# The second half of an input on ScalarE's DMA queue, and neighbouring channel blocks in one PSUM bank

## The chip, the core and the metric

The kernel runs on one core of a Trainium2 chip. The metric is the time of one execution on the device, in microseconds (us); the median of three runs of the kernel before is 260.43 us, with 260.27 and 260.7 us as the lowest and the highest. The engines are called PE (TensorE, matrix products), ACT (ScalarE), DVE (VectorE), POOL (GpSimd) and SP (SyncE, which issues transfers here). PE writes its results to PSUM, which ACT and DVE read; a bank of PSUM holds 512 fp32 values for each of 128 partitions.

## What is computed

The reference is one layer of an encoder block on an input `x` of 256 tokens by 1024 channels, in fp32. Cut to what matters:

```python
h = _rmsnorm(x, norm_gain)                 # x * rsqrt(mean(x*x) + eps) * gain
z = h @ w_in                               # 1024 x 8192, one combined projection
a_in, a_gate, q, k, v, b_gp, g_logits = jnp.split(z, splits, axis=-1)
y_a = (_multiscale_pool(a_in, w_pool, pool_scale) * silu(a_gate)) @ w_proj_a
y_b = (_dilated_attention(q, k, v, rel_bias) * silu(b_gp)) @ w_proj_b
merged = sigmoid(g[0]) * y_a + sigmoid(g[1]) * y_b
y = _rmsnorm(x + merged @ w_out, final_gain)
```

The change lies in what leads up to the first product `h @ w_in`: the load of `x`, its norm, and its transposition to channels by tokens.

## The kernel before, in words

Every fp32 product is made as three products of parts: a matrix is cut into a rounded high part and the rest (`hh` and `hl` for the activations, `whi` and `wlo` for weights), and `hh*whi`, `hl*whi` and `hh*wlo` are accumulated in PSUM. The weights come in 1 MB blocks `wraw` (256 output columns by 8 blocks of 128 input channels), four of them in flight, all issued by SP. ACT makes `whi` by a copy (L128), DVE makes `wlo` by a subtraction (L133).

The head of the program, the part that the change touches, runs before any of the projections and goes like this.

1. SP issues the two halves of `X` (128 tokens by 1024 channels each, L70), then weight block 0 in two halves (L110), weight block 1, the table `oh` and weight block 2 (L112, L147). ACT's queue carries one small transfer, `prm` (L78), with the norm's gains among others.
2. PE runs matmuls on zeros (L179) meanwhile. For each half b of the tokens ACT and DVE square and sum half of the channels each (L185, L187), DVE adds the two sums (L190), and POOL raises the result to -0.5 (L191). Then DVE and ACT scale half of the channels each: XN, channels 0 to 511 by DVE (L194), 512 to 1023 by ACT (L195).
3. DVE makes `whi` of weight block 0 in two copies (L197), each when its half has landed, and POOL makes its `wlo` in two pieces (L163).
4. PE turns XN in 16 pieces of 128 by 128 (`turn`, L204): block `kc` of the channels, half `b` of the tokens. The results go to four tiles `tps`, each one PSUM bank with room for two blocks of channels by 256 tokens.
5. For each block `kc` from 0 to 7 ACT reads the turned block from PSUM, times the gain, and writes `hh[kc]` (L223); then DVE reads the same block and writes `hl[kc] = block * gain - hh[kc]` (L224). PE multiplies as these come (`part0`, L213): pass A is `hh[kc]*whi`, two matmuls for each block, pass B is `hl*whi`, two blocks behind, and pass C is `hh*wlo`, which comes when A and B are through. In the midst of C stand six small matmuls on `oh` (L237).

The part from 2 to 5 stands in a hand-written order: ACT, DVE, PE and POOL carry out their instructions in the order of the code. What a semaphore must be waited for is worked out by the framework from the tiles that instructions touch; for PSUM it orders two engines that touch the same tile, two readers as well.

After the head PE goes through the projections, three matmuls for each block and output (L247, L248, L249), from line 247 on without a break; the pieces of attention are mixed in between.

Of the kernel before, what the change touches and what calls it, by code (L numbers as in the profile page):

```python
# [17 lines left out]
P = 128  # L18
# [24 lines left out]
def encoder_block(ctx: ExitStack, tc: tile.TileContext, x, w_in, lines, w_pool, w_proj_a, w_proj_b,  # L43
                  w_out, final_gain, params, out):
    nc = tc.nc
    x2 = x[0]
# [6 lines left out]
    def slot(shape, dt, tag, name, bufs=1):  # L53
        return sb.tile(shape, dt, tag=tag, name=name, bufs=bufs)
# [6 lines left out]
    def bank(shape, tag, name, bufs):  # L61
        return ps.tile(shape, F32, tag=tag, name=name, bufs=bufs)
# [4 lines left out]

    X = slot([P, 2, D], F32, "v", "X", 2)
    for b in range(2):
        nc.sync.dma_start(X[:, b, :], x2[b * P:(b + 1) * P, :])  # L70
    ident = sb.tile([P, P], F32, name="ident")
    make_identity(nc, ident)
    mhalf = sb.tile([P, 1], F32, name="mhalf")
# [62 lines left out]
    def cut_next():  # L136
        cut_half()
        cut_half()
# [16 lines left out]
    XN = slot([P, 2, D], F32, "v", "XN", 2)  # L155
# [5 lines left out]
    def cut_lo(n, k0, k1, eng):  # L161
        t, (hi, lo) = raws[n][0], parts[n]
        return eng.tensor_tensor(lo[:, k0:k1, :], t[:, k0:k1, :], hi[:, k0:k1, :].bitcast(F32), op=ALU.subtract)  # L163

    def open_parts(n):
        shp = raws[n][1]
        parts[n] = (slot([P] + shp, F32R, "whi", f"whi{n}", 3), slot([P] + shp, F32R, "wlo", f"wlo{n}", 3))
        state["cut"] = 2 * n + 2

    with tc.manual_schedule(engines={mybir.EngineType.Activation, mybir.EngineType.DVE, mybir.EngineType.PE,  # L170
                                    mybir.EngineType.Pool}):
        tiny = sb.tile([P, 1], F32, name="tiny")
        warm = sb.tile([P, P], F32, name="warm")
        nc.vector.memset(warm, 0.0)
        nc.scalar.activation(tiny, warm[:, 0:1], AF.Square)

        def keep_warm(times):
            for _ in range(times):
                nc.tensor.matmul(misc[:, P:2 * P], warm, warm, start=True, stop=True)  # L179

        keep_warm(WARM)
        halves = [slice(h * 512, (h + 1) * 512) for h in range(2)]
        for b in range(2):
            sq = [slot([P, 512], F32, "st", f"sq{b}{h}", 3) for h in range(2)]
            nc.scalar.activation(sq[0], X[:, b, halves[0]], AF.Square, scale=1.0 / 32.0, accum_out=ss[:, b, 0:1])  # L185
            xb = X[:, b, halves[1]]
            nc.vector.tensor_tensor_reduce(sq[1], xb, xb, scale=1.0 / D, scalar=EPS, op0=ALU.mult, op1=ALU.add,  # L187
                                           accum_out=ss[:, b, 1:2])
            t = slot([P, 1], F32, "rt", f"rt{b}", 2)
            nc.vector.tensor_tensor(t, ss[:, b, 0:1], ss[:, b, 1:2], op=ALU.add)  # L190
            nc.gpsimd.tensor_tensor(rs[:, b:b + 1], t, mhalf, op=ALU.pow)  # L191
        open_parts(0)
        for b in range(2):
            nc.vector.tensor_scalar(XN[:, b, halves[0]], X[:, b, halves[0]], rs[:, b:b + 1], None, op0=ALU.mult)  # L194
            nc.scalar.activation(XN[:, b, halves[1]], X[:, b, halves[1]], AF.Copy, scale=rs[:, b:b + 1])  # L195
        for k in (0, 4):
            nc.vector.tensor_copy(parts[0][0][:, k:k + 4, :], raws[0][0][:, k:k + 4, :])  # L197

        cut_lo(0, 0, 5, nc.gpsimd)
        first_lo = cut_lo(0, 5, 8, nc.gpsimd)  # L200
        tps = [bank([P, 2, S], "mm" if i < 3 else "T", f"tp{i}", 3 if i < 3 else 2) for i in range(4)]

        def turn(kc, b):
            nc.tensor.transpose(tps[kc % 4][:, kc // 4, b * P:(b + 1) * P], XN[:, b, kc * P:(kc + 1) * P], ident)  # L204

        acc = bank([P, 2, 512], "S", "k00", 1)
        acc0 = [acc[:, u, 0:S] for u in range(2)]

        def part0(kc, x):
            hi_, lo_ = parts[0]  # L210
            for u in range(2):
                c = slice(u * P, (u + 1) * P)
                nc.tensor.matmul(acc0[u], (lo_ if x == 2 else hi_)[:, kc, c], (hl if x == 1 else hh)[:, kc, :],  # L213
                                 start=x == 0 and kc == 0, stop=x == 2 and kc == KC - 1)

        for kc in range(KC):
            turn(kc, 0)
        for kc in range(KC):
            turn(kc // 2 + kc % 2 * 4, 1)
        for kc in range(KC):  # L220
            v = tps[kc % 4][:, kc // 4]
            gcol = prm[:, kc:kc + 1]
            nc.scalar.activation(hh[:, kc, :], v, AF.Copy, scale=gcol)  # L223
            nc.vector.scalar_tensor_tensor(hl[:, kc, :], v, gcol, hh[:, kc, :].bitcast(F32), op0=ALU.mult,  # L224
                                           op1=ALU.subtract)
            part0(kc, 0)
            if kc >= 2:
                part0(kc - 2, 1)
        for kc in (6, 7):
            part0(kc, 1)  # L230
        for kc in range(KC):
            if kc == 5:

                for t in range(3):
                    w = 3 * NH
                    o = 3 * P + t // 2 * w
                    nc.tensor.matmul(misc[:, t * w:(t + 1) * w], oh[:, t * P:(t + 1) * P], oh[:, o:o + w],  # L237
                                     start=True, stop=True)
            part0(kc, 2)
        cut_next()  # L240
        nc.vector.tensor_copy(line.rearrange("p i r h -> p r i h"),
                              misc[:, 0:LROW * NH].rearrange("p (r i h) -> p r i h", i=2, h=4))
        cut_next()
# [579 lines left out]
```

## Time and profile before

| | |
|---|---|
| median of 3 runs | 260.43 us (260.27 to 260.7) |
| the profiled execution's own time | 260.82 us |
| span of its profile | 259.0 us |
| PE busy | 250.4 us, 97% of the span |
| DVE busy | 210.2 us, 81% |
| ACT busy | 164.4 us, 63% |
| POOL busy | 74.5 us, 29% |
| first matmul of the projections (L247) | at 15.83 us |

The span runs from the first to the last instruction of the program; 1.8 us of the execution's own time lie around it. A row of the timeline has the start in us, the duration in us, the engine, the line, the operation, the tiles written and read, the shapes and a count; what stands in brackets at its end is the idle time of the engine just before, with what ended it. Rows of one kind that follow each other on an engine are merged into one row with their count. Buffers' numbers are left out in the profile: all four `tps` tiles are called `tp`.

### The profile page before, as it was taken

Reading aid. Unit: us, or ns where it says so; the run is one execution under the profiler, and the core shown is the slowest. Engines: PE = TensorE matmul, PEld = TensorE weight load, DVE = VectorE, ACT = ScalarE, POOL = GpSimd, SP = SyncE. Lnnn points to the kernel's source line nnn. Section 1 sums busy time; section 2 is a strip of 40 time slices with the busy share of each in tenths; the row PEclk is TensorE's granted clock in tenths of the full one; section 3 lists DMA queues with packets and bytes.
Section 4 is the critical chain, followed back from the end, with each engine's and each line's share of the span. In section 5 each row is a group of like instructions: output and inputs, shape, how many; then the busy total and the mean of one; then the engine's idle time right before and its main releaser. Section 6 shows DMA issues by size and latency. Waiting matters only on the chain.

```text
span 259.0 us, 5482 instructions
## 1 busy us (share of the span) xinstructions
PE 250.4 (97%) x2160; PEld 248.8 (96%) x2160; DVE 210.2 (81%) x412; ACT 164.4 (63%) x285; POOL 74.5 (29%) x101
## 2 busy tenths in 40 slices
PE   7899999999999999999999999999999999999990
PEld 7899999999999999999999999999999999999990
DVE  2899988778888787889697997967859988899383
ACT  4878577565666565658967777765457797446141
POOL 1563386002798000010763910000010020442011
PEclk9999999999999999999999999999999999999998
DMA  6999999984445553444989867144440696300022
GB/s 231 393 412 363 239 323 329 313 306 162 166 162 172 235 172 156 162 164 162 284 254 257 278 216 273 47 164 162 164 162 6 209 383 233 148 4 0 0 84 81
DMA packets 9992, 52.01 MB, mean 201 GB/s; under 512 B 1147, under 2 KB 2142, under 8 KB 4718
## 3 DMA queue, kind: packets, MB, share of 16 engines
q1 hardware_dynamic: 7022, 44.08, 48.4%
q0 software_dynamic: 2512, 7.12, 11.1%
q10 hardware_dynamic: 432, 0.46, 0.5%
q8 instruction: 17, 0.28, 0.4%
q14 instruction: 9, 0.07, 0.1%
HBM read 47.42 MB, written 1.09 MB: 187 GB/s over the span
## 4 chain that ended last, share of the span: by engine, by line
PE 84%; DVE 6%; issue 3%; ACT 2%; DMA 2%; POOLq 0%; POOL 0%; SPq 0%; DVEq 0%; ACTq 0%
PE v L249 4%; PE v L248 4%; PE q L249 4%; PE q L248 4%; PE v L247 4%; PE q L247 4%; PE g L247 4%; PE g L248 4%; PE g L249 4%; PE k L247 4%; PE k L249 4%; PE k L248 4%; PE y L247 2%; PE y L248 2%; PE y L249 2%
## 5 line engine op out<-in xcount | busy, mean ns | idle before, releaser
L133 DVE TENSOR_TENSOR wlo<-wraw,whi 128x512 fp32r<-128x512 f32 (+2 forms) x134 | 108.5, 849 | 8.3 <-ACT whi L128 7.3
L128 ACT ACTIVATE whi<-wraw 128x1024 fp32r<-128x1024 f32 (+1 forms) x80 | 81.0, 1038 | 23.2 <-PE q L248 10.1
L247 PE MATMUL g<-hh,whi 128*128 128x256 f32 x128 | 35.8, 280 | 0.0
L249 PE MATMUL g<-hh,wlo 128*128 128x256 f32 x128 | 35.4, 277 | 0.0
L248 PE MATMUL g<-hl,whi 128*128 128x256 f32 x128 | 35.4, 276 | 0.0
L304 ACT ACTIVATE st<-st,nm 128x512 f32<-128x512 f32 x16 | 11.6, 722 | 29.6 <-DVE nm L301 29.6
L247 PE MATMUL v<-whi,hh 128*128 128x256 f32 x96 | 26.6, 277 | 0.0
L249 PE MATMUL v<-whi,hl 128*128 128x256 f32 x96 | 26.5, 276 | 0.0
L248 PE MATMUL v<-wlo,hh 128*128 128x256 f32 x96 | 26.5, 276 | 0.0
L249 PE MATMUL q<-hh,wlo 128*128 128x256 f32 x96 | 26.5, 276 | 0.0
L247 PE MATMUL q<-hh,whi 128*128 128x256 f32 x96 | 26.5, 276 | 0.0
L248 PE MATMUL q<-hl,whi 128*128 128x256 f32 x96 | 26.5, 276 | 0.0
L247 PEld LDWEIGHTS g<-hh,whi 128*128 128x128 f32 x128 | 24.0, 188 | 0.1
L248 PEld LDWEIGHTS g<-hl,whi 128*128 128x128 f32 x128 | 24.1, 188 | 0.0
L249 PEld LDWEIGHTS g<-hh,wlo 128*128 128x128 f32 x128 | 24.0, 188 | 0.0
L247 PE MATMUL k<-hh,whi 128*128 128x256 f32 x80 | 22.2, 277 | 0.0
L249 PE MATMUL k<-hh,wlo 128*128 128x256 f32 x80 | 22.1, 277 | 0.0
L248 PE MATMUL k<-hl,whi 128*128 128x256 f32 x80 | 22.1, 277 | 0.0
L248 PEld LDWEIGHTS v<-wlo,hh 128*128 128x128 f32 x96 | 18.0, 188 | 0.0
L249 PEld LDWEIGHTS q<-hh,wlo 128*128 128x128 f32 x96 | 18.0, 188 | 0.0
L248 PEld LDWEIGHTS q<-hl,whi 128*128 128x128 f32 x96 | 18.0, 188 | 0.0
L247 PEld LDWEIGHTS q<-hh,whi 128*128 128x128 f32 x96 | 18.0, 188 | 0.0
(177 smaller groups left out, 760.2 us busy)
## 6 DMA issues: line engine op xcount, KB each, us to landing
wraw<-in_w_in_dram SPq DMA_DIRECT2D x31, 1024.0 KB, 6.4
wraw<-in_w_out_dram SPq DMA_DIRECT2D x4, 1024.0 KB, 4.9
T<-line_d POOLq DMA_DIRECT2D x4, 576.0 KB, 6.8
KX<-KX POOLq DMA_DIRECT2D x8, 256.0 KB, 14.5
wraw<-in_w_proj_a_dram SPq DMA_DIRECT2D x2, 1024.0 KB, 4.7
wraw<-in_w_proj_b_dram SPq DMA_DIRECT2D x2, 1024.0 KB, 4.9
X<-in_x_dram SPq DMA_DIRECT2D x2, 512.0 KB, 4.2
wraw<-in_w_in_dram SPq DMA_DIRECT2D x2, 512.0 KB, 6.6
```

Source lines behind the costliest of these rows:

```text
L128: nc.scalar.activation(hi[:, s, :], t[:, s, :], AF.Copy)
L133: nc.vector.tensor_tensor(lo[:, s, :], t[:, s, :], hi[:, s, :].bitcast(F32), op=ALU.subtract)
L247: nc.tensor.matmul(acc, ah, bh, start=first, stop=False)
L248: nc.tensor.matmul(acc, ah, bl, start=False, stop=False)
L249: nc.tensor.matmul(acc, al, bh, start=False, stop=last)
L304: e = nc.scalar.activation(st, st, AF.Exp, bias=nm, scale=-1.0, accum_out=l)
```

## The change

Three lines. The load of the second half of `X` is issued by ACT's queue, ahead of `prm`, where it was issued by SP. And the turned blocks are laid out otherwise in the four banks: before, block `kc` shared its bank with block `kc + 4` (`tps[kc % 4]`), now blocks 0 and 1 share the first bank, 2 and 3 the second, and so on (`tps[kc // 2]`). The pieces of the second half of the tokens are turned in the order 0, 1, 2, ... 7, where the order was 0, 4, 1, 5, 2, 6, 3, 7. The order in which ACT and DVE read the blocks is 0 to 7 in both.

```diff
     for b in range(2):
-        nc.sync.dma_start(X[:, b, :], x2[b * P:(b + 1) * P, :])
+        (nc.sync, nc.scalar)[b].dma_start(X[:, b, :], x2[b * P:(b + 1) * P, :])
...
         def turn(kc, b):
-            nc.tensor.transpose(tps[kc % 4][:, kc // 4, b * P:(b + 1) * P], XN[:, b, kc * P:(kc + 1) * P], ident)
+            nc.tensor.transpose(tps[kc // 2][:, kc % 2, b * P:(b + 1) * P], XN[:, b, kc * P:(kc + 1) * P], ident)
...
         for kc in range(KC):
             turn(kc, 0)
         for kc in range(KC):
-            turn(kc // 2 + kc % 2 * 4, 1)
+            turn(kc, 1)
         for kc in range(KC):
-            v = tps[kc % 4][:, kc // 4]
+            v = tps[kc // 2][:, kc % 2]
             gcol = prm[:, kc:kc + 1]
             nc.scalar.activation(hh[:, kc, :], v, AF.Copy, scale=gcol)
             nc.vector.scalar_tensor_tensor(hl[:, kc, :], v, gcol, hh[:, kc, :].bitcast(F32), op0=ALU.mult,
                                            op1=ALU.subtract)
             part0(kc, 0)
             if kc >= 2:
                 part0(kc - 2, 1)
```

ACT's eight reads of the turned blocks, in the program's order, before; `tp_138` to `tp_141` are the four banks `tps[0]` to `tps[3]`, and what an instruction waits for stands in brackets (`PE_49`, `DVE_49`: the semaphore that PE or DVE raises; `DMAHW`: a transfer):

```order
L223 ACTIVATE hh<-tp_138,prm 128x256 [waits DMAHW0_49,PE_49]
L223 ACTIVATE hh<-tp_139,prm 128x256 [waits PE_49]
L223 ACTIVATE hh<-tp_140,prm 128x256 [waits PE_49]
L223 ACTIVATE hh<-tp_141,prm 128x256 [waits PE_49]
L223 ACTIVATE hh<-tp_138,prm 128x256 [waits DVE_49]
L223 ACTIVATE hh<-tp_139,prm 128x256 [waits DVE_49]
L223 ACTIVATE hh<-tp_140,prm 128x256 [waits DVE_49]
L223 ACTIVATE hh<-tp_141,prm 128x256 [waits DVE_49]
```

And the same eight reads now:

```order
L223 ACTIVATE hh<-tp_138,prm 128x256 [waits DMAHW2_49,PE_49]
L223 ACTIVATE hh<-tp_138,prm 128x256 [waits DVE_49]
L223 ACTIVATE hh<-tp_139,prm 128x256 [waits PE_49]
L223 ACTIVATE hh<-tp_139,prm 128x256 [waits DVE_49]
L223 ACTIVATE hh<-tp_140,prm 128x256 [waits PE_49]
L223 ACTIVATE hh<-tp_140,prm 128x256 [waits DVE_49]
L223 ACTIVATE hh<-tp_141,prm 128x256 [waits PE_49]
L223 ACTIVATE hh<-tp_141,prm 128x256 [waits DVE_49]
```

The second read of a bank waits for DVE in both; it stood four reads after the first, and now it stands directly behind it. Of the eight reads four wait for DVE as before, now blocks 1, 3, 5 and 7 in place of 4, 5, 6 and 7.

PE's transposes of the second half of the tokens before, in which the second row waits for ACT's half of the channels:

```order
L204 MATMUL tp_138<-ident,XN 128x128 [waits DVE_49]
L204 MATMUL tp_138<-ident,XN 128x128 [waits Activation_49]
L204 MATMUL tp_139<-ident,XN 128x128 x2
L204 MATMUL tp_140<-ident,XN 128x128 x2
L204 MATMUL tp_141<-ident,XN 128x128 x2
```

And now:

```order
L204 MATMUL tp_138<-ident,XN 128x128 [waits DVE_49]
L204 MATMUL tp_138<-ident,XN 128x128
L204 MATMUL tp_139<-ident,XN 128x128 x2
L204 MATMUL tp_140<-ident,XN 128x128 [waits Activation_49]
L204 MATMUL tp_140<-ident,XN 128x128
L204 MATMUL tp_141<-ident,XN 128x128 x2
```

The wait for ACT's half of the channels has moved from the second piece to the fifth; the first bank is complete two pieces in, and needs DVE's half of the channels alone.

## The prediction, made before the changed kernel was run

> **What bounds the kernel now.** I read the busy time by stage first, to see whether anything but PE sets the pace after the head (columns: stretch in us, its length, then busy us and instruction count of each engine).
>
> ```profile
> 15.80:60.00 44.20, 44.20 (x392) 44.20 (x391) 37.80 (x56) 30.06 (x52) 15.53 (x19) 1.00 1.02 311
> 60.00:120.00 60.00, 60.00 (x526) 60.00 (x526) 50.33 (x108) 37.71 (x69) 19.82 (x31) 1.00 0.47 168
> 120.00:180.00 60.00, 60.00 (x531) 60.00 (x530) 50.09 (x94) 43.38 (x75) 19.64 (x22) 1.00 0.72 224
> 180.00:205.00 25.00, 24.84 (x214) 24.42 (x213) 20.61 (x49) 16.87 (x32) 0.73 (x1) 1.00 0.35 127
> 205.00:252.00 47.00, 46.86 (x401) 46.53 (x400) 38.61 (x79) 25.07 (x40) 10.23 (x12) 1.00 0.34 124
> ```
>
> From 15.8 us to 252 us PE is idle for 0.30 us (0.16 and 0.14 in the last two rows). So the projections begin when the head lets them, and everything behind that moment moves with it: other engines feed PE but are released by PE's own results, and at most 0.3 us of a delay can be swallowed. A microsecond of the head is a microsecond of the kernel. Now the head, by its chain of waits (start, duration, piece):
>
> ```profile
> 1.17 4.61 DMA X<-in_x_dram
> 5.80 0.69 DVE sq L187
> 6.60 0.16 DVE rt L190
> 6.76 0.41 DVE XN L194
> 7.21 2.15 PE tp L204 x16
> 9.36 5.28 PE k L213 x42
> 14.64 0.58 PE misc L237 x6
> 15.22 0.77 PE k L213 x6
> ```
>
> X's second half lands at 5.80, the norm and the transposes follow, and from 9.36 on PE works through the 48 matmuls of weight block 0 without a break that the chain would show. ACT and DVE feed it just fast enough. Their single instructions, of the timeline:
>
> ```profile
> 8.74 0.47 ACT L223 ACTIVATE hh<-tp,prm 128x256 fp32r<-128x256 f32 x1 [0.42 <-PE tp L204]
> 9.12 0.47 ACT L223 ACTIVATE hh<-tp,prm 128x256 fp32r<-128x256 f32 x1
> 9.10 0.69 DVE L197 CAST whi<-wraw 128x1024 fp32r<-128x1024 f32 x1 [0.41 <-DMA wraw<-in_w_in_dram]
> 9.71 0.48 DVE L224 SCALAR_TENSOR_TENSOR hl<-tp,prm,hh 128x256 fp32r<-128x256 f32 x1
> 10.22 0.48 ACT L223 ACTIVATE hh<-tp,prm 128x256 fp32r<-128x256 f32 x1
> 10.10 0.47 DVE L224 SCALAR_TENSOR_TENSOR hl<-tp,prm,hh 128x256 fp32r<-128x256 f32 x1
> 10.61 0.47 ACT L223 ACTIVATE hh<-tp,prm 128x256 fp32r<-128x256 f32 x1
> 12.45 0.48 DVE L224 SCALAR_TENSOR_TENSOR hl<-tp,prm,hh 128x256 fp32r<-128x256 f32 x1
> 13.08 0.41 PE L213 MATMUL k<-hl,whi 128*128 128x256 f32 x2
> 15.83 0.28 PE L247 MATMUL k<-hh,whi 128*128 128x256 f32 x1
> ```
>
> The first two rows are hh of blocks 0 and 1, 0.37 us apart. DVE's first hl comes late, at 9.71, since the copy of weight block 0's second half stands ahead of it and waited for its transfer until 9.10. The decisive reading is in the next four rows. hh of block 4 starts at 10.22; hl of block 0 ends at 9.71 + 0.48 = 10.19. hh of block 5 starts at 10.61; hl of block 1 ends at 10.10 + 0.47 = 10.57. Blocks 0 and 4 share a bank, and so do 1 and 5: **ACT's read of the second block of a bank starts 0.03 us after DVE's read of the first has ended.** The two readers of one bank are kept apart by a real wait, and in this layout it costs nothing, because four reads lie between. hl of block 7 starts at 12.45 and ends at 12.93; PE's last two matmuls of pass B, which need it, start at 13.08, a little behind, and pass C and the six small matmuls take it to 15.83.
>
> **The change part by part.** *The banks.* Now block 1 shares its bank with block 0, so hh of block 1 waits for hl of block 0, which itself waits for hh of block 0: ACT and DVE take turns instead of overlapping. The same holds for 3, 5 and 7. DVE after ACT costs the same hand-over as ACT after DVE, which a weight block's cut shows:
>
> ```profile
> 32.24 1.06 ACT L128 ACTIVATE whi<-wraw 128x1024 fp32r<-128x1024 f32 x1 [1.65 <-PE q L248]
> 33.33 1.78 DVE L133 TENSOR_TENSOR wlo<-wraw,whi 128x1024 fp32r<-128x1024 f32 x1 [0.48 <-ACT whi L128]
> ```
>
> 32.24 + 1.06 = 33.30, and DVE starts at 33.33: 0.03 us. From hh of one odd block to that of the next the chain is: hh odd 0.48, hand-over 0.03, then hl odd, and hl even 0.39 behind it (the spacing of DVE's reads, 10.10 - 9.71; the hh even that it needs started 0.37 after hh odd and is done by then), hl even 0.48, hand-over 0.03. That makes **1.41 us for two blocks**, where before two blocks took 2 x 0.39 = 0.78.
>
> Counted out: hl of block 0 from 9.71 to 10.19; hh of block 1 at 10.22, of block 3 at 11.63, of block 5 at 13.04, of block 7 at 14.45, done at 14.93. (hl of block 7 starts 0.48 + 0.03 later, at 14.96, and ends at 15.44; before it ended at 12.93, so ACT and DVE are 2.5 us later.) PE now waits for most of this time. Its last eight matmuls of passes A and B are, in the code's order, two on hh of block 7, then the pairs on hl of blocks 5, 6 and 7. The first starts 0.05 us after 14.93 (a hand-over to PE: XN ends at 6.76 + 0.41 = 7.17, PE starts at 7.21), at 14.98. The first matmul after a wait takes 0.22 us until the next:
>
> ```profile
> 9.27 0.39 PE L213 MATMUL k<-hh,whi 128*128 128x256 f32 x1
> 9.49 0.53 PE L213 MATMUL k<-hh,whi 128*128 128x256 f32 x2
> ```
>
> The others follow 0.113 us apart (392 matmuls in 44.2 us of the first table). So the pair on hl of block 7 starts at 14.98 + 0.22 + 5 x 0.113 = 15.77, behind 15.44, in place of 13.08: 2.69 us later. Behind it pass C and the six small matmuls follow as before, if the weights are there. POOL's wlo of block 0 is done at 9.87 + 4.79 = 14.66:
>
> ```profile
> 9.87 4.79 POOL L163 TENSOR_TENSOR wlo<-wraw,whi 128x1280 fp32r<-128x1280 f32 x2 [2.30 <-DVE whi L197]
> 11.77 1.06 ACT L128 ACTIVATE whi<-wraw 128x1024 fp32r<-128x1024 f32 x1
> 12.87 2.86 DVE L133 TENSOR_TENSOR wlo<-wraw,whi 128x1024 fp32r<-128x1024 f32 x1
> 20.08 1.23 DVE L133 TENSOR_TENSOR wlo<-wraw,whi 128x1024 fp32r<-128x1024 f32 x1
> ```
>
> So the projections start at 15.83 + 2.69 = 18.52: **+2.7 us**. Queued behind the waiting ACT and DVE are weight block 1's whi (at 11.77 before) and wlo (12.87). whi now starts 0.37 behind hh of block 7, at about 14.8, and its first half is done at 15.9, so wlo starts at 15.9. In before it took 2.86 us beside POOL's work; at that it would end at 18.8, next to its first use, the third matmul behind 18.52. POOL is through at 14.66, though, and a piece of that size by itself takes 1.23, so it ends at 17.2. I count nothing for it, at worst 0.1 us.
>
> *The earlier transposes.* Bank 0 is complete after two pieces instead of needing ACT's half of the channels. In the rows above that is worth about 0.1 us for hh of block 0 (PE's second piece waited for ACT's XN). It is worth nothing at the end: hl of block 0 starts at 9.71 for the weights' sake, and hh of block 0 is done at 9.21, 0.5 us before.
>
> *The load of X.* The issue on SP costs about 0.43 us each, so X's second half and the weights behind it are issued 0.43 us earlier:
>
> ```profile
> 0.74 0.85 SPq L70 DMA_DIRECT2D X<-in_x_dram  x2
> 0.74 0.41 ACTq L78 DMA_DIRECT2D prm<-in_params_dram  x1
> 4.50 0.63 ACT L185 ACTIVATE sq<-X 128x512 f32<-128x512 f32 x1 [1.82 <-DMA X<-in_x_dram]
> 4.50:5.00 0.50, 0.50 (x7) 0.50 (x6) 0.50 (x1) 0.50 (x1) 0.00 (x0) 1.00 1.03 418
> ```
>
> But X lands 4.50 and 5.80, 1.3 us apart and not 0.43, and the transfer engines are full between (share 1.03): bytes set the landing, not the issue. On two queues the halves share those engines, so the first can come later, by up to 1.3 us, and the second hardly earlier. The Trainium skill, "DMA: Bandwidth & Descriptors", section "Issuing engines are not separate DMA queues", says just this: transfers of several engines run on the same 16 and interleave, and only issue time is saved; by it this part gains nothing. The delay is covered up to 0.5 us by the slack of hl of block 0 just named. The weights of block 0, which set hl's start, have the same bytes ahead of them as before. I take zero, between -0.43 (they land as much earlier as they are issued; hh of block 0 then nearly binds) and +0.45 (the late case below). On ACT the second issue delays what follows by 0.41 us, inside the 1.82 us that ACT waits for X: nothing.
>
> **The sum.** Against the profiled execution's own time 260.82 (span 259.0, 1.8 around it): 260.82 + 2.7 = 263.5. The median of the runs is 0.39 below the profiled execution, so **263.1 us** is the time I give. With the bounds of the load, the wlo piece and the 0.3 us of idle time that could swallow some: 2.7 - 0.43 - 0.3 and 2.7 + 0.45 + 0.1, that is 262.4 to 263.7; I give 262.3 to 263.8.
>
> **The rivals.**
>
> *The first half of X lands as late as the second* (5.80). DVE's work on one half takes from 5.80 to 6.60 + 0.16, so that the second half's starts 0.9 us later than now, and with it the norm, the copies of L197 and hh. Of these 0.9 the 0.5 of slack are covered; hl of block 0 starts some 0.45 us later: 263.6 us. For it: the full transfer engines. Against: X's head start on SP's queue.
>
> *The clock of PE falls.* PE is busy about half of the time from 9.3 to 15.5. If the clock is taken back for that, matmuls go at half pace until it is granted again; at the start of the program the slow pace lasted some 3 us (9 matmuls in the 2 us after 1.0, 18 in the 2 us after 4.0).
>
> ```profile
> 1.00:3.00 2.00, 1.95 (x9) 1.95 (x10) 0.00 (x0) 1.49 (x2) 0.29 (x1) 1.00 0.48 123
> 4.00:6.00 2.00, 2.00 (x18) 1.84 (x17) 1.06 (x4) 0.93 (x3) 0.38 (x1) 1.00 1.01 371
> 253.00:254.00 1.00, 0.00 (x0) 0.00 (x0) 0.96 (x4) 0.00 (x0) 0.02 (x1) 1.00 0.00 0
> 256.00:257.00 1.00, 0.00 (x0) 0.00 (x0) 0.00 (x0) 0.00 (x0) 0.00 (x0) 0.76 1.02 365
> ```
>
> Three microseconds at half pace lose 1.5: 264.6 us. Against it: at the end the clock holds at 1.00 through a wholly idle PE and falls only after 256, over 3 us after the last matmul; the longest idle piece here is 1.4 us. The Trainium skill, "TensorE: Matmul & The Clock Gate", section "What's actually happening", names an idle window of about 3.4 us; by that it doesn't happen.
>
> *The other side: ACT does not wait, and the head starts earlier.* If the guard were on addresses, block 1 would be free to be read while DVE reads block 0. Then the earlier issue and the earlier transposes are all that is left: 0.43 + 0.12, to 259.9 us. It decides if hh of block 1 starts within 0.4 us of block 0's. Against it: blocks 0 and 4 have disjoint addresses too, and the rows above show that wait. The Trainium skill, "PSUM — Partial Sum Buffer", section "PSUM bank collisions raise a hardware error", says that two engines must not be in one bank at once, reads included, and that software has to keep them apart.
>
> *It does not matter:* the delay is swallowed later, 260.4 us. Against it stand the 0.30 us of idle PE.
>
> **How the numbers follow.** Forecast 0.82, the late half 0.06, the clock 0.05, the other side 0.04, swallowed 0.03. The range 262.3 to 263.8 holds the first two. Changes within 0.2% (0.5 us) can't be told from none; so faster 0.04, same 0.03, slower 0.93.
>
> **What would show it.** In the changed profile: hh of block 1 starts 0.03 us behind the end of hl of block 0; the eight hh instructions stretch over about 6.2 us, in place of the 3.13 of the row below, which is before's; the first L247 stands near 18.5; PE has idle time between 9.5 and 15.5, released by ACT and DVE, and none to speak of later. The row of before:
>
> ```profile
> 8.74 3.13 ACT L223 ACTIVATE hh<-tp,prm 128x256 fp32r<-128x256 f32 x8 [0.42 <-PE tp L204]
> ```
>
> It is wrong if they still take 3.1 us, if L247 starts before 17.5, or if it starts late and the span doesn't grow by as much.

## The result and the profile after

The changed kernel takes 263.77 us (median of 5 runs, 263.35 to 264.59) where the kernel before takes 260.70 us (median of 5 runs, 260.27 to 260.97); the ratio is 1.0124, with a 95% interval of 1.0108 to 1.0139. It is slower by 3.1 us. In another set of runs it took 263.42 us against 260.78, 2.6 us more (ratio 1.0106, 1.0093 to 1.0119). The profiled execution took 263.35 us, with a span of 261.6 us.

ACT's and DVE's reads of the turned blocks in the changed kernel, by the timeline; the brackets hold the idle time ahead of a row's first instruction and what ended it:

```profile
9.69 0.47 ACT L223 ACTIVATE hh<-tp,prm 128x256 fp32r<-128x256 f32 x1 [0.55 <-PE tp L204]
10.71 0.84 ACT L223 ACTIVATE hh<-tp,prm 128x256 fp32r<-128x256 f32 x2 [0.55 <-DVE hl L224]
12.12 0.84 ACT L223 ACTIVATE hh<-tp,prm 128x256 fp32r<-128x256 f32 x2 [0.58 <-DVE hl L224]
13.54 0.84 ACT L223 ACTIVATE hh<-tp,prm 128x256 fp32r<-128x256 f32 x2 [0.58 <-DVE hl L224]
14.96 0.47 ACT L223 ACTIVATE hh<-tp,prm 128x256 fp32r<-128x256 f32 x1 [0.58 <-DVE hl L224]
10.19 0.48 DVE L224 SCALAR_TENSOR_TENSOR hl<-tp,prm,hh 128x256 fp32r<-128x256 f32 x1
11.22 0.87 DVE L224 SCALAR_TENSOR_TENSOR hl<-tp,prm,hh 128x256 fp32r<-128x256 f32 x2 [0.54 <-ACT hh L223]
15.46 0.48 DVE L224 SCALAR_TENSOR_TENSOR hl<-tp,prm,hh 128x256 fp32r<-128x256 f32 x1 [0.54 <-ACT hh L223]
19.01 0.28 PE L247 MATMUL k<-hh,whi 128*128 128x256 f32 x1
```

What was one unbroken row of eight before is broken into 1, 2, 2, 2 and 1, and each row behind the first follows an idle half microsecond that DVE ended; DVE's rows are broken by ACT in the same way. hh of block 1 starts at 10.71, 0.04 behind the end of hl of block 0 (10.19 + 0.48). From odd block to odd block it is 12.12 - 10.71 = 1.41 and 13.54 - 12.12 = 1.42 us. The first matmul of the projections stands at 19.01, where it stood at 15.83: 3.18 us later.

PE's waits in the changed kernel (what waited and for what; total us, times, longest):

```profile
PE tp L204 <- DVE XN L194: 2.1, 1, 2.1
PE k L213 <- ACT hh L223: 1.3, 4, 0.5
PE misc L179 <- DVE warm L174: 1.1, 1, 1.1
PE op L330 <- DVE ATT L346: 0.2, 1, 0.2
```

The busy time by stretches in the changed kernel, in the rest of the head and in the stages behind it (the first busy figure is PE's, the 1.00 near the end is its granted clock):

```profile
10.30:18.50 8.20, 6.91 (x51) 6.04 (x51) 5.57 (x10) 6.06 (x11) 5.57 (x6) 1.00 1.02 398
18.50:60.00 41.50, 41.50 (x368) 41.50 (x368) 34.35 (x52) 28.54 (x47) 14.61 (x19) 1.00 1.00 279
```

Two waits are new or longer: PE waits for hh, four times, and for XN 2.1 us in place of 1.2. Behind the head PE is as busy as before. The longer wait for XN goes back to the load of X. Here is the chain of waits of the changed kernel up to the first turns:

```profile
0.74 5.01 DMA X<-in_x_dram
...
5.77 0.69 DVE sq L187
...
6.90 0.87 POOL rs L191
...
7.79 0.50 DVE XN L194
...
8.34 1.32 PE tp L204 x10
...
9.69 0.48 ACT hh L223
```

The first half of X is seen at 5.77; before it was 4.50, and the chain went through the second half. The trace's packets show why: from 3.0 to 4.5 us SP's queue moved 71 packets with 0.29 MB and ACT's 73 with 0.30 MB, so the two halves of X came side by side. Before, SP's queue moved 0.56 MB in the same stretch, and ACT's 0.05 MB of `prm`.

### The profile page after: what moved, and what is told of

Its sections match the earlier page's. It is cut to its first block, busy times and chain, and to the rows that moved or that the text cites. A ratio compares the mean times of both kernels' runs of the same rounds, so it can differ in the third digit from the quotient of the medians.

```text
span 261.6 us, 5482 instructions
## 1 busy us (share of the span) xinstructions
PE 250.7 (96%) x2160; PEld 248.5 (95%) x2160; DVE 208.9 (80%) x412; ACT 164.4 (63%) x285; POOL 74.0 (28%) x101
## 4 chain that ended last, share of the span: by engine, by line
PE 81%; DVE 7%; issue 3%; ACT 3%; DMA 2%; POOL 1%; POOLq 0%; DVEq 0%; ACTq 0%
PE v L249 4%; PE q L248 4%; PE v L248 4%; PE v L247 4%; PE q L249 4%; PE q L247 4%; PE g L247 4%; PE g L248 4%; PE g L249 4%; PE k L247 3%; PE k L249 3%; PE k L248 3%; PE y L247 2%; PE y L248 2%; PE y L249 2%
## 5 line engine op out<-in xcount | busy, mean ns | idle before, releaser
L133 DVE TENSOR_TENSOR wlo<-wraw,whi 128x512 fp32r<-128x512 f32 (+2 forms) x134 | 106.8, 836 | 10.0 <-ACT whi L128 9.2
L247 PEld LDWEIGHTS v<-whi,hh 128*128 128x128 f32 x96 | 18.0, 188 | 0.0
L249 PEld LDWEIGHTS v<-whi,hl 128*128 128x128 f32 x96 | 18.0, 188 | 0.0
```

The source lines that it names most:

```text
L133: nc.vector.tensor_tensor(lo[:, s, :], t[:, s, :], hi[:, s, :].bitcast(F32), op=ALU.subtract)
L247: nc.tensor.matmul(acc, ah, bh, start=first, stop=False)
L249: nc.tensor.matmul(acc, al, bh, start=False, stop=last)
```

## The experiments

The theory after this profile: two losses, each by itself. **Turns on a bank**: an ACT read right behind DVE's read of the same bank waits for it, which makes 1.41 us of two blocks. **The load of X**: with its halves on two queues their packets take turns on the same transfer engines, the first half lands late, and what hangs on it moves. The rivals: that X's load is most of it; or that the sharing of a bank costs in another way than by the order of the reads (PE's writes of neighbours, say). The waits that make the turns are semaphores that the framework puts in for the two readers of a tile; no run leaves them out, so nothing here tells what the chip does without them. In the kernel with another read order and in those that load each half of X over both queues, the line numbers shown are one higher.

**The banks alone**, as an edit of the changed kernel:

```diff
-        (nc.sync, nc.scalar)[b].dma_start(X[:, b, :], x2[b * P:(b + 1) * P, :])
+        nc.sync.dma_start(X[:, b, :], x2[b * P:(b + 1) * P, :])
```

> The new banks and transposes, both halves of X on SP as before. Theory (ACT and DVE take turns on a shared bank; X's load is a separate cost): hl of block 0 starts at 9.7 as in before, two blocks take 1.42 us, the first L247 starts at 18.5, 2.7 us later than before, and the time is 2.7 us over before, near 263.2. Rival (X's load is most of it): hl of block 0 is on time but the first L247 starts by 17, and the time is under 262.

It took 263.18 us against 260.60, 2.6 us more (ratio 1.0103, 1.0084 to 1.0122). Its timeline:

```profile
10.19 0.84 ACT L223 ACTIVATE hh<-tp,prm 128x256 fp32r<-128x256 f32 x2 [1.06 <-DVE hl L224]
11.61 0.84 ACT L223 ACTIVATE hh<-tp,prm 128x256 fp32r<-128x256 f32 x2 [0.58 <-DVE hl L224]
9.68 0.48 DVE L224 SCALAR_TENSOR_TENSOR hl<-tp,prm,hh 128x256 fp32r<-128x256 f32 x1
18.49 0.28 PE L247 MATMUL k<-hh,whi 128*128 128x256 f32 x1
```

hl of block 0 starts at 9.68, where it was 9.71, the period is 1.42, and the projections begin at 18.49, 2.66 us later than before; 2.69 had been worked out. The banks carry most of the loss. One of the four runs, at 263.47, has a mean granted clock of 0.986, below the kernel before's 0.992 to 0.998, so part of its time may be the clock's; the profiled one has 0.997.

**The load alone**, as an edit of the kernel before:

```diff
-        nc.sync.dma_start(X[:, b, :], x2[b * P:(b + 1) * P, :])
+        (nc.sync, nc.scalar)[b].dma_start(X[:, b, :], x2[b * P:(b + 1) * P, :])
```

> X's second half on ACT's queue, the banks as before. Theory: the first half of X is seen at 5.77 in place of 4.50, hh of block 0 starts at 9.7 in place of 8.74, and as PE is the bound of the head in this layout, the first L247 moves by the same 0.94 us to 16.8; time 0.6 to 0.9 us over before, near 261.4. Rival (the late half costs only the 0.49 us by which hl of block 0 was late in the changed kernel): first L247 at 16.3, time 0.5 over before. Rival (X's load is most of the change's loss): 2 us or more.

It took 260.98 us against 260.60, 0.4 us more (ratio 1.0022, 1.0004 to 1.0040; single runs from 260.61 to 262.90, and the profile is of the fastest):

```profile
5.29 0.63 ACT L185 ACTIVATE sq<-X 128x512 f32<-128x512 f32 x1 [2.13 <-DMA X<-in_x_dram]
9.20 3.03 ACT L223 ACTIVATE hh<-tp,prm 128x256 fp32r<-128x256 f32 x8 [0.56 <-PE tp L204]
9.33 0.70 DVE L197 CAST whi<-wraw 128x1024 fp32r<-128x1024 f32 x1 [0.37 <-DMA wraw<-in_w_in_dram]
16.24 0.28 PE L247 MATMUL k<-hh,whi 128*128 128x256 f32 x1
```

The first half of X came at 5.29, later than before's 4.50 but earlier than the changed kernel's 5.77, so hh moved by 0.46 us and the projections by 0.41. That PE passes on the delay of hh nearly whole in this layout agrees with the theory; the size expected, 0.94, would have needed X at 5.77. The weights of block 0 came later too, at 9.33 in place of 9.10. The result lies nearer to the rival's numbers, 16.3 and 0.5 us, but not by its cause: hl of block 0, at 9.94, was only 0.23 us late.

**Banks shared by blocks two apart**, as an edit of the kernel before (the expressions go on to the right as they were):

```diff
-            nc.tensor.transpose(tps[kc % 4][:, kc // 4, b * P:(b + 1) * P], ...
+            nc.tensor.transpose(tps[kc // 4 * 2 + kc % 2][:, kc // 2 % 2, b * P:(b + 1) * P], ...
-            turn(kc // 2 + kc % 2 * 4, 1)
+            turn((0, 2, 1, 3, 4, 6, 5, 7)[kc], 1)
-            v = tps[kc % 4][:, kc // 4]
+            v = tps[kc // 4 * 2 + kc % 2][:, kc // 2 % 2]
```

> Banks shared by blocks two apart (0 and 2, 1 and 3, 4 and 6, 5 and 7), read in the order 0 to 7, X on SP as before. Theory (the cost comes from how few reads lie between the two blocks of a bank): hh of block 2 waits for hl of block 0 until 10.2, hh of block 6 for hl of block 4, two stops in place of four turns; first L247 near 16.5, 0.7 us later than before, time near 261.3. Rival (any layout other than before's is as costly as the changed kernel's): first L247 near 18.5.

It took 261.19 us against 260.60, 0.6 us more (ratio 1.0025, 1.0014 to 1.0036):

```profile
8.61 0.84 ACT L223 ACTIVATE hh<-tp,prm 128x256 fp32r<-128x256 f32 x2 [0.30 <-PE tp L204]
10.21 1.59 ACT L223 ACTIVATE hh<-tp,prm 128x256 fp32r<-128x256 f32 x4 [0.76 <-DVE hl L224]
12.02 0.86 ACT L223 ACTIVATE hh<-tp,prm 128x256 fp32r<-128x256 f32 x2 [0.21 <-DVE hl L224]
16.52 0.28 PE L247 MATMUL k<-hh,whi 128*128 128x256 f32 x1
```

Two stops, at blocks 2 and 6, and the projections at 16.52. One step apart costs 2.66 us, two 0.69, four nothing: the loss follows the distance between the reads of a bank.

**The changed kernel's banks in another read order**, as an edit of the kernel with the banks alone:

```diff
-        for kc in range(KC):
+        reads = (0, 2, 4, 6, 1, 3, 5, 7)
+        for n_, kc in enumerate(reads):
...
-            if kc >= 2:
-                part0(kc - 2, 1)
-        for kc in (6, 7):
+            if n_ >= 2:
+                part0(reads[n_ - 2], 1)
+        for kc in reads[6:]:
```

> The changed kernel's banks (neighbours share) and its transposes, but ACT, DVE and PE take the blocks in the order 0, 2, 4, 6, 1, 3, 5, 7; X on SP as before. Theory: what costs is reading the two blocks of a bank directly after each other, so with four reads between them the eight hh take 3.1 us again, the first L247 starts at 15.7 to 15.9 and the time is before's within 0.3 us. Rival (the shared bank itself or PE's writes of neighbours into it cost): the eight hh take 5 us or more and the time is 2 us over before.

It took 260.80 us against 260.60 (ratio 1.0010, 1.0000 to 1.0020), the 2.6 us of the banks are gone:

```profile
8.61 3.24 ACT L224 ACTIVATE hh<-tp,prm 128x256 fp32r<-128x256 f32 x8 [0.29 <-PE tp L204]
9.69 3.22 DVE L225 SCALAR_TENSOR_TENSOR hl<-tp,prm,hh 128x256 fp32r<-128x256 f32 x8
15.79 0.28 PE L248 MATMUL k<-hh,whi 128*128 128x256 f32 x1
```

The same blocks share the same banks and PE writes them in the same order; the reads of one bank now stand four apart, and PE multiplies in the order of the reads. Neither the shared bank nor PE's writes cost anything that can be told here. It also shows the transposes' gain at work and lost: hh of block 0 starts at 8.61 in place of 8.74, and hl of block 0 at 9.69 all the same.

**The changed kernel once more**, for the part that had been 3.18 - 2.66 = 0.52 us.

> The changed kernel once more. Theory: the first L247 follows hl of block 0 by 8.81 us, and hl of block 0 starts at 9.70 (for the weights) or 4.42 us after X's first half is seen, whichever is later. With X's first half seen anywhere from 5.2 to 5.8 that is 18.5 to 19.0 and a time of 263.2 to 263.8. Rival (the rest of the loss over the banks' has another place than X's load): an early X and still a first L247 at 19.0 or later.

It took 263.42 us against 260.78. X's first half was seen at 5.38, so by the theory hl of block 0 should have started at 9.80; it started at 10.01, and the projections at 18.83, which is 8.82 behind it, as expected:

```profile
5.38 0.63 ACT L185 ACTIVATE sq<-X 128x512 f32<-128x512 f32 x1 [2.23 <-DMA X<-in_x_dram]
9.40 0.69 DVE L197 CAST whi<-wraw 128x1024 fp32r<-128x1024 f32 x1 [0.35 <-DMA wraw<-in_w_in_dram]
10.01 0.48 DVE L224 SCALAR_TENSOR_TENSOR hl<-tp,prm,hh 128x256 fp32r<-128x256 f32 x1
18.83 0.28 PE L247 MATMUL k<-hh,whi 128*128 128x256 f32 x1
```

So the small part has two doors: in the first profile the late X held hl of block 0, in this one the weights did, whose second half was seen at 9.40 in place of 9.10. I had written the weights down as unmoved. A likely cause is `prm`: it now stands behind X on ACT's queue and lands 7.0 us after its issue, where it took 3.9, so its packets now run beside those of weight block 0. From 5.5 to 8.0 us of this profile they take 8.8% of the transfer engines' time, and SP's queue moves 0.69 MB, where before it had the stretch for itself and moved 0.77. That this makes the 0.3 us was not tested by itself.

**X's second half behind `prm`**, as an edit of the kernel before:

```diff
-        nc.sync.dma_start(X[:, b, :], x2[b * P:(b + 1) * P, :])
+    nc.sync.dma_start(X[:, 0, :], x2[0:P, :])
...
     nc.scalar.dma_start(prm, params)
+    nc.scalar.dma_start(X[:, 1, :], x2[P:2 * P, :])
```

> Banks as before, X's second half on ACT's queue, but issued behind prm, some 0.45 us later. Theory (turns with the second half's packets delay the first): fewer packets of the first half are left when the second half's begin, so the first is seen between 4.6 and 5.2, earlier than the 5.28 and 5.77 of the two kernels that issue it ahead of prm, and the first L247 starts at 15.8 to 16.1. Rival (the issue order on ACT does not matter): the first half is seen at 5.3 or later.

The first half came early, at 4.51, as the theory has it and more. But I had not followed the second half, and it now took turns with weight block 0 instead: from 4.5 to 7.0 us ACT's queue moved 0.42 MB and SP's 0.38. By the chain of waits it took 7.10 us from its issue and was seen at 8.30:

```profile
1.18 7.10 DMA X<-in_x_dram
...
8.30 0.69 DVE sq L187
...
9.71 2.40 PE tp L204 x10
```

It took 264.16 us against 260.78, 3.4 us more (ratio 1.0134, 1.0109 to 1.0159), and the projections began at 19.46, where 15.8 to 16.1 had been expected. PE's first turns by the timeline, and then the busy time in the stretch around them (PE first, the granted clock third from the end):

```profile
9.71 3.50 PE L204 MATMUL tp<-ident,XN 128*128 128x128 f32 x16 [2.67 <-DVE XN L194]
```

```profile
9.48:12.89 3.41, 3.18 (x15) 3.18 (x16) 2.10 (x5) 1.62 (x4) 1.60 (x2) 0.50 1.03 394
```

PE stood idle for 2.67 us, from 7.04 on. Its clock fell to half 2.44 us into that, at 9.48, and came back 3.41 us later, so that the 16 transposes took 3.50 us. This is what the rival of the falling clock spoke of, in a kernel that idles longer: in the changed kernel PE idles for 2.05 us at this place (a row of its timeline has the 16 transposes at 8.34 for 1.97 us), and the clock holds. The Trainium skill, "TensorE: Matmul & The Clock Gate", section "What's actually happening", has a window of about 3.4 us that runs freely and doesn't start with the work; the 3.41 us until the clock came back agree with its length. So do the other traces: the first change of the granted clock stands between 3.87 and 6.33 us, and from one change to the next it is 1, 2 or 72 to 75 times 3.41 us in all of them. Three of the four runs of this kernel have a mean granted clock of 0.983 to 0.987, and those of the kernel before lie at 0.992 to 0.998. The length of an idle piece alone does not decide when the clock falls, as the next kernel shows; whether the phase of the window does, these runs don't tell.

**Each half of X over both queues.** If turns are the cause, the two queues should work on the same half at the same time. As an edit of the kernel before:

```diff
-        nc.sync.dma_start(X[:, b, :], x2[b * P:(b + 1) * P, :])
+        for q, eng in enumerate((nc.sync, nc.scalar)):
+            eng.dma_start(X[:, b, q * 512:(q + 1) * 512], x2[b * P:(b + 1) * P, q * 512:(q + 1) * 512])
```

> Banks as before. Each half of the tokens is loaded in two pieces of 512 channels, one issued by SP and one by ACT, first half of the tokens first; prm behind them on ACT. Theory (in the changed kernel X's first half is late because its packets take turns with those of the second half on the same 16 transfer engines): now all packets that run beside the first half belong to it, so it is seen at 4.2 to 4.6 and the second at 5.6 to 5.9, the first L247 starts at 15.6 to 15.9 and the time is before's within 0.3 us. Rival (ACT's queue itself starts late or is slow): the first half is seen after 5.0 and the first L247 after 16.1.

X itself did as the theory says: its first pieces were used from 3.82 and 4.06 and the second half's from 5.22 and 5.41, all earlier than before. But the kernel took 261.69 us against 260.78 (ratio 1.0051, 1.0026 to 1.0076; single runs from 260.77 to 264.37). Its profiled execution is the slowest, at 264.37 us, with the projections at 18.89, where 15.6 to 15.9 had been expected. Its chain, as the profile infers it, runs through `prm`:

```profile
1.66 7.81 DMA prm<-in_params_dram
9.55 1.58 ACT hh L224 x4
11.13 0.48 DVE hl L225
```

ACT's first read needs the gains, and `prm`, now the last on ACT's queue, lands 7.81 us after its issue. The chain passes over two things that weigh more. One is the weights of block 0; the other, in the busy time from 10.30 to 18.50 us, is PE's clock, at a mean of 0.79:

```profile
10.51 0.69 DVE L198 CAST whi<-wraw 128x1024 fp32r<-128x1024 f32 x1 [0.56 <-DMA wraw<-in_w_in_dram]
```

```profile
10.30:18.50 8.20, 7.86 (x51) 7.52 (x51) 7.31 (x13) 6.25 (x11) 5.91 (x8) 0.79 1.00 357
```

hh of block 0 was done at 10.02 and could not hold hl of block 0 until 11.12; the second copy of the weights did, which began 1.41 us later than before (10.51 for 9.10), with hl 0.61 us behind its start as before. And from 11.75 to 15.16 us, 3.41 us again, the clock was at half, though PE's longest idle piece ahead of it was 1.06 us. The 36 matmuls of weight block 0 that follow took 6.04 us, and 4.42 in the next kernel, whose clock held. 1.41 and 1.62 make up 3.03 of the 3.06 us by which the projections were late. PE had been busy for 2.01 of the 3.41 us before this fall, and for 0.97 before the fall in the kernel with X behind `prm`; in the changed kernel it was busy for only 1.81 of such 3.41 us, from 4.48, where its clock changes first, to 7.89, and the clock held. What decides it stays open, and so does how many of the other runs had such a fall.

**The same with `prm` on SP**, between X and weight block 0, as an edit of the kernel just above; and then, as an edit of that, also with hl of block 0 read ahead of DVE's second copy of the weights:

```diff
-    nc.scalar.dma_start(prm, params)
+    nc.sync.dma_start(prm, params)
```

> Banks as before; each half of X in two pieces over SP and ACT, and prm on SP between X and weight block 0, so that no small transfer stands last on ACT's queue. Theory (transfers that share the engines take turns packet by packet, and what lands last is what had to take turns longest): X is seen at 3.8 to 4.1 and 5.2 to 5.5, prm before 7, weight block 0 at 8.9 to 9.4; the first L247 starts at 15.3 to 15.8 and the time is before's or up to 0.5 us below. Rival (two queues are a loss in themselves): weight block 0 after 9.8, the first L247 after 16.2, time over 261.2.

```diff
-        for k in (0, 4):
-            nc.vector.tensor_copy(parts[0][0][:, k:k + 4, :], raws[0][0][:, k:k + 4, :])
-        cut_lo(0, 0, 5, nc.gpsimd)
-        first_lo = cut_lo(0, 5, 8, nc.gpsimd)
+        nc.vector.tensor_copy(parts[0][0][:, 0:4, :], raws[0][0][:, 0:4, :])
...
             part0(kc, 0)
+            if kc == 0:
+                nc.vector.tensor_copy(parts[0][0][:, 4:8, :], raws[0][0][:, 4:8, :])
+                cut_lo(0, 0, 5, nc.gpsimd)
+                first_lo = cut_lo(0, 5, 8, nc.gpsimd)
```

> As x_each_prm_sp, and DVE reads hl of block 0 before its second copy of weight block 0 in place of after it. Theory: hl of block 0 starts at 8.8 to 9.3 and no longer waits for the weights; as PE is the bound from about 10 on, the first L247 starts at 15.2 to 15.6, time up to 0.6 us below before's. Rival (hl of block 0 was never on the path in this layout): the same first L247 as x_each_prm_sp.

They took 261.37 and 261.74 us against 260.64 (ratios 1.0038, 1.0025 to 1.0052, and 1.0062, 1.0038 to 1.0086). Again X was early (first pieces at 3.98 and 4.22 in the first of the two), and again something behind it was late: in the first the second half of weight block 0, seen at 10.13 in place of 9.10, in the second weight block 1, on which PE itself waited at 14.39. In that kernel PE's order has two matmuls of the projections ahead of the last two of pass B and of all of pass C, and their wait held up the rest; the projections go on at 17.46. hl of block 0 did start early there, at 9.48, but what that is worth can't be told behind this wait. From the chain of each:

```profile
2.58 7.53 DMA wraw<-in_w_in_dram
```

```profile
3.06 10.19 DMA wraw<-in_w_in_dram
13.27 1.07 ACT whi L129
14.39 0.38 PE k L248
```

What the transfers moved from 1 to 10 us, in 40 equal slices, before and in the first of the two:

```profile
GB/s 0 0 0 182 255 91 55 150 364 396 444 414 369 412 437 400 437 400 401 346 291 291 218 237 182 237 273 364 437 437 419 473 473 455 437 437 400 437 400 437
```

```profile
GB/s 0 0 0 82 64 118 300 410 391 391 428 392 373 328 391 419 382 292 137 41 141 91 109 182 309 291 382 364 310 455 364 528 346 437 510 437 492 291 601 328
```

Both have a hole behind X, from about 5 to 7 us, and it is deeper with X in smaller pieces on two queues (41 to 141 GB/s against 182 to 291 at its worst). For the first of the two this is the rival's result, with weight block 0 after 9.8 and the projections at 16.88: the form in which I tried it is a loss in itself. Why the hole is there, and why it deepens, no run here settles. No version beat the kernel before.

## Why the prediction was right or wrong

**Right: the mechanism, the place and most of the size.** The term of the banks, 2.69 us at the first matmul of the projections, measured 2.66 with the banks alone; the period of 1.41 us measured 1.41 and 1.42, the hand-over 0.03 to 0.04. PE's new idle time came in the head alone, 1.3 us of it in waits for hh and 0.9 more ahead of the turns, which the load of X explains. The runs that move the reads apart without moving the banks, or the banks without the reads, tie it to the order of the reads.

**Right: the cover of weight block 1's cuts and of the transposes.** Pass C ran without a break, and hh of block 0 was earlier by 0.08 to 0.13 us where X was on time, with nothing gained at the end.

**Wrong: "I take zero" for the load of X.** This is the mis-sized term. In the changed kernel hl of block 0 started at 10.19 and 10.01 in its two profiles, 0.48 and 0.30 us late, and the projections at 19.01 and 18.83 in place of the 18.52 worked out. The step that failed is the cover: a delay of up to 1.3 us was allowed for, a slack of 0.5 us set against it, and nothing taken for what was left. The slack had to cover a first half of X that came 5.77 - 4.50 = 1.27 us late in the first profile, of which 0.95 reached hh of block 0 (9.69 for 8.74). The rival "the first half of X lands as late as the second" is what that profile shows, at +0.48 where 0.45 had been given for it, though I had left it a chance of only 0.06. And the assumption that the weights of block 0 "have the same bytes ahead of them as before" did not keep them at their time: 9.40 for 9.10 in the second profile, which set hl there. By itself the load costs 0.41 us at the projections, and 0.4 in the medians.

**Wrong by a smaller term: "The median of the runs is 0.39 below the profiled execution".** That came from three runs. In the larger sets the kernel before has medians of 260.70 and 260.78, not 260.43, and the changed kernel's medians are 0.42 and 0.18 above its profiled executions. The medians came out 0.67 and 0.32 us above the forecast of 263.1; 0.27 and 0.35 of that is the kernel before. The rise, which the forecast puts at 2.67, was 3.07 and 2.64. In the second set the rise agrees by luck: the head was 3.00 us late, 0.31 more than worked out, and the medians do not show that part. The intervals of the changed kernel and of the banks alone overlap; the load's part in the changed kernel is read from the traces, not from the times.

**Right, with an allowance: a microsecond of the head is a microsecond of the kernel.** Set side by side matmul by matmul, the 3.18 us of the first profile are still 3.17 at 191 us. The span rose by 2.53 only (259.04 to 261.57), for a reason far behind the head that the last section describes. That the profiled 263.35 us lies so near to the 263.5 of the sum is luck: 0.49 more in the head, and 0.65 less behind it.

**Wrong in its reasons: the rival of the clock.** The clock did not fall in the two profiles of the changed kernel (1.00 in the rows of the head), but the argument against it does not hold. PE's longest idle piece in the head was 2.05 us, where 1.4 had been named. In two other kernels the clock fell 2.44 us into an idle piece, and with no piece longer than 1.06 us ahead of it, both less than the 3 us and more from which I had argued. That it held is luck as far as these runs tell. The other two rivals did not come: no later stage swallowed the delay in a wait of PE, and X's first half was seen later, not earlier.

## What to carry to other kernels

When two engines read the same bank one after the other, look at how many reads lie between: far enough apart the wait is free, next to each other it turns two overlapped streams into one serial chain, and a change of layout that looks neutral pays for it (here 1.41 us for 0.78). Such a wait can be read in the trace of the kernel before, as a start that stands a constant 0.03 us behind another engine's end. Before a load is moved to another queue, follow every transfer that stands behind it on either queue, small ones too: in every load tried here that used both queues for X something landed later, X itself, `prm` or the weights.

## What the runs showed that was not expected

Matmuls of the projections do not always follow each other at the same pace at full granted clock. The same 12 us of the program (3 us later in the changed kernel), before and after, by stretches:

```profile
214.00:226.00 12.00, 12.00 (x104) 12.00 (x103) 10.12 (x21) 6.80 (x10) 2.86 (x3) 1.00 0.54 197
```

```profile
217.00:229.00 12.00, 12.00 (x108) 12.00 (x107) 10.38 (x21) 7.07 (x10) 2.85 (x3) 1.00 0.55 200
```

104 matmuls in one profile and 108 in the other, both with PE busy throughout and the clock at 1.00. With the matmuls of the two traces set side by side in their order, this makes the changed kernel 0.5 us faster between 210 and 229 us, and another 0.1 goes between 191 and 196. It does not come from the change. The kernel with the banks alone has the slow stretch as the kernel before has it:

```profile
217.00:229.00 12.00, 12.00 (x105) 12.00 (x104) 10.12 (x21) 6.82 (x10) 2.86 (x3) 1.00 0.56 198
```

So have the kernels with banks two apart and with X behind `prm`; the ones with the load alone and with another read order have the quicker pace. The cause stays open. It bounds what a single profiled execution can tell about a few tenths of a microsecond: the load alone has a span 0.2 us shorter than before's with its projections 0.41 us later. The place of the first projection matmul told it better than the span.
